# More attention tiles turned by VectorE and DRAM in a hybrid streaming encoder layer, with the halves of the output joined later

## The chip, the cores and the metric

The kernel runs on one core of a Trainium2 chip, in fp32 throughout (TensorE multiplies in the one-pass fp32r format, with every operand split into a high and a low part). The metric is the device time of one execution in microseconds. The profile is that of one execution.

## The reference

One layer of a streaming encoder is computed for a prompt of 1024 frames and a sample chunk of 32 frames, model width 1024. The part that matters here:

```python
u = rmsnorm(h, g_pre) @ w_in
qa, ka, va, ga, qb, kb, vb, gb = jnp.split(u, SPLIT_IDX, axis=-1)
# mixer A, 8 heads of 64: softmax over a band of 8 earlier chunks of 64, with a clipped relative bias
w = jax.nn.softmax(s + bias, axis=-1);  oA = w @ v
# mixer B, 8 heads of 64: stick breaking, strictly causal
w = exp(log_sigmoid(z) + after);        oB = w @ v
y = concat(oA * silu(ga), oB * silu(gb)) @ w_out
h = h + rmsnorm(y, g_post)
h = h + sigmoid(h @ w_ple_gate) * (p @ w_ple)
```

Outputs are the new rows for both groups and the new keys and values.

## The kernel before, in words

**Stages.** First the rows are normalized and turned (`first` stage, to about 40 us). Then come eight stages, one for each pair of heads, in the order A0, B0, A1, B1, A2, B2, A3, B3. In each, the attention of that pair is woven with dense work: the projection columns (`mm_k`, `mm_q`, `mm_v`) of the pair after it, and in the last stage all eight gate columns (`mm_gA`, `mm_gB`). Sample attention runs in stages 2, 3, 6 and 7. After about 600 us the two output products (`o...P`, `g...P`) run, seven half-size products in place of eight.

**One head of attention** (`attention`, L838) has eight query tiles of 128 rows. Tile i of A sees key blocks max(0, i-4) to i (at most 5), tile i of B blocks 0 to i. For each tile, `scores` (L873) multiplies queries by keys (high and low part) into PSUM. For A, a custom VectorE instruction adds the bias and takes the minimum, ScalarE takes the exponential and its row sum, VectorE takes 1/sum, and GpSimd multiplies the row by it (L908 to L910). For B, ScalarE takes two sigmoids, VectorE runs the product scan and GpSimd multiplies. The weights then lie with queries on partitions in a ring called `be`; the product with the values wants keys there. `weights_t` (L919) turns them. Most tiles are turned by TensorE, 128x128 blocks at a time (`ptw`); ScalarE then copies the high part to the ring `wTh` and VectorE subtracts to get the low part in `wTl`. The tiles in `ROUND` (L38), 5 of A and 4 and 6 of B, go round by DRAM instead: VectorE turns 32x32 squares from `be` into the ring `om` (L941), one DMA writes them to a DRAM scratch `swap`, four DMAs read them back into `be` (L946), ScalarE copies the high part and VectorE subtracts (L951, L952). `values` (L969) then multiplies with the value rows for tiles 0-3 and for tiles 4-7 (`PV`); a matmul's moving operand is cut from the ring in runs of 128 elements, one for each tile that sees the block (`Segments`, L166). Its 128 output rows are two halves of 64 that belong together; ScalarE copies one half and VectorE adds the other (L986, L987), and a DMA stores the sum to `o_dr`.

**Gates.** `col_steps` (L770) loads `o_dr` and multiplies it by silu of the gate (L803), in three chunks of 352 columns per gate, and stores to `og_dr`.

**Sums of weights.** `sum_weights` (L1365) forms sums of quarters of the two output weight matrices on GpSimd (tiles named `oB` and `gB` in the profile) and stores them; `SUMS_AT` (L1353) puts them in stages 2, 4, 5 and 6.

**What sets the order.** Every instruction is recorded, then `Recorder.order` (L393) lists them by a simulated schedule: each engine takes the ready instruction with the lowest key; the key is the program position plus an offset from the table `AHEAD_OF` (L28, applied at L351) by engine and name of the tile written. Each engine runs its list strictly in order, and all DMAs are issued by one queue, that of SyncE (SP). All instructions are emitted from L473, so the profile's line is the same for all and the tile names tell them apart. The stream of tiles (`attention_stream`, L1287) emits scores, then two tiles later the turn (`LAG_T`), and the value product with the turn of its last tile (`LAG_V`).

Of the kernel before, what the change touches and what calls it, by code (L numbers as in the profile page):

```python
# [26 lines left out]
NT = 9  # L27
AHEAD_OF = {  # L28
    ('ACT', 'o'): -25, ('ACT', 'oT'): 100, ('ACT', 'w'): -400, ('ACT', 'x'): -75,
    ('DVE', 'newh'): 200, ('DVE', 'sq'): -400, ('POOL', 'bias'): -50, ('POOL', 'kl'): 100,  # L30
    ('POOL', 'ksS'): -50, ('POOL', 'om'): -50, ('POOL', 'qsS'): 100, ('SP', 'be'): 25,
    ('SP', 'biass'): 200, ('SP', 'kl'): 50, ('SP', 'ogg'): -400, ('SP', 'pp'): -400,
    ('SP', 'stv'): -100, ('SP', 'vns'): -25,
# [4 lines left out]
ROUND = {"A": ((5,),), "B": ((4,),(6,))}  # L38
# [127 lines left out]
class Segments:  # L166


    def __init__(self, buf, start, step, n):
        self.buf, self.start, self.step, self.n = buf, start, step, n  # L170
        self.shape = [buf.shape[0], n, P]
        self.box = (buf.box[0], (start, start + (n - 1) * step + P))

    def get(self):
        base = self.buf.get()[:, self.start:self.start + P]
        return bass.AP(tensor=base.tensor, offset=base.offset, ap=[base.ap[0], [self.step, self.n], [1, P]])

    def free(self):
        return self.n * P


class Op:
    __slots__ = ("eng", "what", "args", "kw", "key", "busy", "late", "ready", "left", "after", "at", "size", "shared", "table")
# [89 lines left out]
class Recorder:  # L273


    def __init__(self):
        self.with_table, self.old_table = [], []
        self.ops, self.cls, self.low, self.closed, self.turns = [], 0, 0, [], []
# [31 lines left out]
    def node(self, eng, what, args, kw, after):  # L310
        o = Op()
        o.eng, o.what, o.args, o.kw, o.after = eng, what, args, kw, after
        o.key = (self.cls if eng == "PE" else self.low, len(self.ops))
        o.shared, o.table = False, None
# [3 lines left out]
    def add(self, eng, what, args, kw):  # L318
# [29 lines left out]
        if eng != "PE" and writes:  # L348
            name = str(writes[0].buf.name)
            kind = (eng, name[:next((i for i, x in enumerate(name) if x.isdigit() or x in "AB_"), len(name))])  # L350
            o.key = (o.key[0], o.key[1] + AHEAD_OF.get(kind, 0))  # L351
# [7 lines left out]
    def cost(eng, method, args, kw, writes, reads):  # L359
# [8 lines left out]
        if eng == "ACT":  # L368
            return (165 if psum else 200) + 0.83 * n + (190 if "accum_out" in kw else 0), 0
        if eng == "DVE":  # L370
# [6 lines left out]
            return 155 + 1.04 * n + (83 if method == "tensor_tensor_reduce" else 0), 0  # L377
        if eng == "POOL":
            if method == "tensor_tensor":
                if n == 1:  # L380
                    return 400, 0
                return 190 + (1.77 if out.buf.dtype == F32 else 2.15) * n, 0
# [10 lines left out]
    def order(self):  # L393
# [17 lines left out]
        while len(out) < len(self.ops):  # L411
# [24 lines left out]
            if e == "CTL":  # L436
                done = t
# [41 lines left out]
def stream_step(  # L479
# [22 lines left out]
    o_dr = [scratch([P, T], f"o_dr{n}") for n in range(8)]  # L502
# [34 lines left out]
    ring0, ring1 = Arena(rec, at, "om", 3076), Arena(rec, at, "be", 3640)  # L537
# [126 lines left out]

    KDh, KLD, Lq, V2 = {}, {}, {}, {}
# [104 lines left out]
    def col_steps(j):  # L770
# [7 lines left out]
        def mms(c, part):  # L778
# [20 lines left out]
            if k == "g":  # L799
# [3 lines left out]
                nc.gpsimd.tensor_tensor(sg, sg, box["og"], ALU.mult)  # L803
# [34 lines left out]
    def attention(ab, p, h):  # L838
# [5 lines left out]
        def begin():  # L844
            if ab == "A":
# [4 lines left out]
                box["bias"] = bias  # L850

        def lo_block(i):
            return max(0, i - 4) if ab == "A" else 0

        together = {i: g for g in ROUND[ab] for i in g}
        whole, done_with = {}, []
# [4 lines left out]
        def rooms(i):  # L861

            more = ab == "B"
            g = together.get(i, (i,))
            if g not in whole:
                n = sum(cost(x) for x in g) * P
                whole[g] = ring0.tile([P, n + more * len(g)], f"om{nm}_{i}"), ring1.tile([P, n], f"be{nm}_{i}")
            k, n = g.index(i), cost(i) * P
            a = sum(cost(x) for x in g[:k]) * P
            w0, w1 = whole[g]  # L870
            return w0[:, a + more * k:a + more * k + n + more], w1[:, a:a + n]

        def scores(i):  # L873
# [27 lines left out]
            else:  # L901
# [12 lines left out]

        LAID = {("A", 0): (3, 13), ("A", 1): (4, 20), ("B", 0): (3, 13), ("B", 1): (7, 29)}

        def weights_t(i):  # L919
            g = i // 4  # L920
            step, size = LAID[ab, g]
            if g not in wT:
                wT[g] = [x.tile([P, size * P], f"{x.name}{nm}_{g}") for x in (ringh, ringl)]
            b0 = lo_block(i)
            w0, w1 = state.pop(i)
            n = i + 1 - b0
            at_ = ((i - 4 * g) * step + b0) * P
            hi, lo = (x[:, at_:at_ + n * P] for x in wT[g])
            if i in together:

                group = together[i]
                done_with.append((i, hi, lo))
                if i != group[-1]:
                    return
                w0, w1 = whole[group]
                m = sum(cost(x) for x in group)
# [996 lines left out]
```

## Time and profile before

| | |
|---|---|
| three runs, median (lowest to highest) | 793.03 us (788.52 to 793.21) |
| the profiled execution, span | 790.1 us |
| TensorE busy | 772.5 us (98%) |
| VectorE, ScalarE, GpSimd busy | 599.7, 529.0, 474.9 us |
| mean granted TensorE clock | 0.996 |
| DMA | 154.71 MB, mean 196 GB/s |
| chain that ended last | TensorE 90%, DMA 3%, VectorE 2%, GpSimd 2% |

A row of a group of instructions reads: line, engine, operation, tile written <- tiles read, shapes, count, then the total busy time and the mean time of one, then the idle time of the engine just before them and what ended it. In a timeline a row gives the start, the duration of a merged run of equal instructions and, in brackets, an idle time before it with its releaser. Matmuls overlap in the array, so what one costs is the distance from its start to the start of the next, not its duration.

### The profile page before, as it was taken

The page shows a single profiled execution, that of the slowest core. Times are in us where ns is not written, and L with a number is a line of the kernel's source. Part 1 is how long each engine was busy: PE and PEld are TensorE (multiplying, and loading weights), DVE is VectorE, ACT ScalarE, POOL GpSimd, SP SyncE. Part 2 cuts the span into 40 slices and gives each one's busy share as a digit, 9 for nine tenths or more (in the row PEclk, how much of TensorE's full clock was granted, in tenths as well). Part 3 has the DMA queues.
Part 4 walks back from the last instruction along what each step waited for, and adds up shares of the span by engine and source line. Part 5 has one row for each costly group of instructions (what it writes and reads, how often), then busy time and mean ns, then how long its engine had stood idle before and what let it go on. Part 6 is the DMA issues. An engine that isn't in the chain of part 4 may idle for free.

```text
span 790.1 us, 14436 instructions
## 1 busy us (share of the span) xinstructions
PE 772.5 (98%) x4534; PEld 714.0 (90%) x4534; DVE 599.7 (76%) x1127; ACT 529.0 (67%) x1146; POOL 474.9 (60%) x551
## 2 busy tenths in 40 slices
PE   8999999999999999989999999999999999999997
PEld 7999999999989999979999999999998787888786
DVE  7728757797788888768788788868575587988965
ACT  5647775777677767767767777664446867777651
POOL 5636634574575457757778678566473339599523
PEclk9999999999999999989999999999999999999999
DMA  9646634647676639655857877886489766859754
GB/s 300 227 133 181 142 98 138 148 110 224 162 200 162 158 111 245 165 173 158 226 157 222 196 229 217 211 227 188 142 281 288 244 212 212 271 162 353 268 160 134
DMA packets 184542, 154.71 MB, mean 196 GB/s; under 512 B 64705, under 2 KB 150505, under 8 KB 184466
## 3 DMA queue, kind: packets, MB, share of 16 engines
q1 hardware_dynamic: 184466, 153.79, 66.6%
q8 instruction: 36, 0.59, 0.3%
q14 instruction: 40, 0.33, 0.1%
HBM read 94.97 MB, written 50.36 MB: 184 GB/s over the span
## 4 chain that ended last, share of the span: by engine, by line
PE 90%; DMA 3%; DVE 2%; POOL 2%; SPq 1%; ACT 1%; issue 1%; POOLq 0%; DVEq 0%; ACTq 0%
PE mm_gB L473 6%; PE mm_gA L473 6%; PE mm_qA L473 6%; PE mm_vA L473 6%; PE mm_kA L473 5%; PE mm_vB L473 5%; PE mm_qB L473 5%; PE mm_kB L473 4%; PE PVB L473 4%; PE SB L473 4%; PE PVA L473 3%; PE SA L473 3%; PE ptwB L473 3%; PE g1P L473 2%; PE o3P L473 2%; PE o1P L473 2%
## 5 line engine op out<-in xcount | busy, mean ns | idle before, releaser
L473 POOL TENSOR_TENSOR be<-be,om 128x256 f32<-128x256 f32 (+8 forms) x66 | 81.5, 1238 | 70.4 <-DVE om L473 32.8
L473 DVE TENSOR_TENSOR_SCAN om<-om,SB 128x384 f32<-128x384 f32 (+5 forms) x96 | 92.4, 967 | 20.1 <-ACT be L473 11.9
L473 POOL TENSOR_SCALAR be<-be,statA 128x640 f32<-128x640 f32 (+3 forms) x64 | 46.4, 732 | 38.0 <-DVE statA L473 26.5
L473 ACT ACTIVATE om<-SB 128x384 f32<-128x384 f32 (+5 forms) x96 | 46.8, 499 | 24.9 <-DVE SB L473 14.4
L473 ACT ACTIVATE be<-SB 128x384 f32<-128x384 f32 (+5 forms) x96 | 46.7, 502 | 7.2 <-DVE om L473 6.2
L473 ACT ACTIVATE be<-om,statA 128x640 f32<-128x640 f32 (+3 forms) x64 | 44.5, 696 | 9.1 <-DVE wTl L473 4.2
L473 ACT CAST wTh<-ptwA 128x512 fp32r<-128x512 f32 (+2 forms) x80 | 31.9, 426 | 18.3 <-PE ptwA L473 17.7
L473 DVE TENSOR_TENSOR wTl<-ptwA,wTh 128x512 fp32r<-128x512 f32 (+2 forms) x80 | 37.0, 483 | 8.7 <-ACT wTh L473 8.0
L473 ACT CAST wTh<-ptwB 128x512 fp32r<-128x512 f32 (+3 forms) x64 | 29.9, 491 | 13.2 <-PE ptwB L473 9.1
L473 DVE TENSOR_TENSOR wTl<-ptwB,wTh 128x512 fp32r<-128x512 f32 (+3 forms) x64 | 33.3, 542 | 6.8 <-ACT wTh L473 6.6
L473 PE MATMUL ptwA<-ident,be 128*128 128x128 f32 x200 | 32.3, 273 | 3.8 <-DVE wlsA L473 1.6
L473 DVE TENSOR_TENSOR wTl<-be,wTh 128x640 fp32r<-128x640 f32 (+1 forms) x24 | 28.7, 1196 | 8.3 <-ACT wTh L473 3.5
L473 PE MATMUL SB<-kdB,LB 128*128 128x384 f32 (+5 forms) x96 | 33.4, 353 | 0.0
L473 PE MATMUL SB<-klB,LB 128*128 128x384 f32 (+5 forms) x96 | 32.5, 343 | 0.0
L473 DVE CUSTOM_DVE_ANT_0 om<-SA,biasA 128x320 f32<-128x320 f32 (+2 forms) x64 | 30.1, 480 | 3.0 <-PE SA L473 2.7
L473 POOL TENSOR_TENSOR oB<-oB,oB 128x256 f32<-128x256 f32 x32 | 25.1, 800 | 9.4 <-DMA oB<-in_w_out_dram 9.4
L473 PE MATMUL SA<-kdA,LA 128*128 128x320 f32 (+2 forms) x96 | 30.6, 322 | 0.0
L473 PE MATMUL SA<-klA,LA 128*128 128x320 f32 (+2 forms) x96 | 29.8, 315 | 0.0
L473 PEld LDWEIGHTS ptwA<-ident,be 128*128 128x128 f32 x200 | 24.5, 141 | 5.4 <-issue 3.0
L473 PE MATMUL ptwB<-ident,be 128*128 128x128 f32 x192 | 29.2, 274 | 0.0
L473 POOL TENSOR_TENSOR gB<-gB,gB 128x256 f32<-128x256 f32 x32 | 27.1, 863 | 3.0 <-DMA gB<-in_w_ple_gate_dram 1.5
L473 POOL TENSOR_TENSOR sggB<-sggB,oggB 128x352 f32<-128x352 f32 x12 | 13.9, 1161 | 20.5 <-DVE sggB L473 18.4
(696 smaller groups left out, 2677.9 us busy)
## 6 DMA issues: line engine op xcount, KB each, us to landing
oB<-in_w_out_dram SPq DMA_DIRECT2D x16, 256.0 KB, 4.0
sum_dro<-oB SPq DMA_DIRECT2D x16, 256.0 KB, 2.3
gB<-in_w_ple_gate_dram SPq DMA_DIRECT2D x16, 256.0 KB, 3.8
sum_drg<-gB SPq DMA_DIRECT2D x16, 256.0 KB, 2.4
x<-in_x_prompt_dram SPq DMA_DIRECT2D x16, 256.0 KB, 4.0
h_dr<-h SPq DMA_DIRECT2D x8, 512.0 KB, 3.4
ht<-h_dr SPq DMA_DIRECT2D x8, 512.0 KB, 4.1
raw<-sum_drg SPq DMA_DIRECT2D x16, 256.0 KB, 3.0
```

The costliest lines, as they stand in the source:

```text
L473: getattr(getattr(tc.nc, o.what[0]), o.what[1])(*args, **kw)
```

## The change

**Which tiles go round by DRAM.** `TURNED` names tiles 5, 6 and 7 of A and 4, 5 and 6 of B. Each head now starts with them (`TILES`: A 5, 6, 7, 4, 0-3; B 6, 7, 5, 4, 0-3; the last head still runs 7 down to 0). Tiles are grouped for the value product by `SETS`: A as before, B in (0-3), (4, 5), (6, 7). The value product of a set that ends before the head does is put one tile later (`LAG_G`).

**Landing in place.** The four reads go straight to their place in the ring `wTl`, not to `be`; ScalarE copies the high part from there to `wTh`, and the low part is subtracted in place, on GpSimd (on VectorE in the last pair). For that, the rings hold tiles 4-7 with the 32-element pieces of one partition group side by side, so a matmul's moving operand is cut from the ring in runs of 32 elements. The A softmax works in `be` in place, without `om`.

**Softmax.** A's row sums of a head go to eight columns of a small tile; one reciprocal per head, and one DMA to `one_dr`. The multiplications by 1/sum go away from the tiles.

**Output halves.** Both halves of `PV` (128 rows) are copied and stored, without the VectorE addition. A gate chunk loads two halves and, for A, 1/sum, joins them by one VectorE addition and for A one more GpSimd product.

**Order.** `AHEAD_OF` has one offset per stage for each of 70 kinds, TensorE's among them; `sum_weights` moves to stages 0, 1, 4 and 5, the sample steps are put elsewhere (`SAMPLE_AT`), and a few assumed durations of the order's model change.

Counted over the whole program, TensorE's 128x128 transposes of weights go from 392 to 264; matmuls of `PVB` go from 192 to 288 with the same number of columns; SP's DMA issues go from 840 to 1024.

```diff
-ROUND = {"A": ((5,),), "B": ((4,),(6,))}
+TURNED = {"A": (5, 6, 7), "B": (4, 5, 6)}
+SETS = {"A": ((0, 1, 2, 3), (4, 5, 6, 7)), "B": ((0, 1, 2, 3), (4, 5), (6, 7))}
+TILES = {"A": (5, 6, 7, 4, 0, 1, 2, 3), "B": (6, 7, 5, 4, 0, 1, 2, 3)}
+LAG_G = 1
 AHEAD_OF = {
...
+    ("DVE", "om"): (0, -37, -327, 0, -219, 382, -149, 7, -419, 0),
...
+    ("PE", "PV"): (0, 0, 0, 0, 123, 284, 0, 0, 0, 0),
...
-    o_dr = [scratch([P, T], f"o_dr{n}") for n in range(8)]
+    o_dr = [scratch([2, P, T], f"o_dr{n}") for n in range(8)]
+    one_dr = [scratch([2, SEQ], f"one_dr{p}") for p in range(4)]
...
-                box["og"] = at2.tile([P, CH], F32, tag="bias", name=f"og{kind}{p}_{c}", bufs=2)
-                dma(box["og"], o_dr[n][:, cs])
...
+                for h in range(2):
+                    rows = slice(h * HD, (h + 1) * HD)
+                    dma(og[rows, 0:2], o_dr[n][h, :, cs].rearrange("(a d) t -> d a t", a=2))
+                    if ab == "A" and j not in early:
+                        dma(box["one"][rows, 0:old], one_src(p, h, c * CH, old))
...
-                nc.gpsimd.tensor_tensor(sg, sg, box["og"], ALU.mult)
+                nc.vector.tensor_tensor(og[:, 0], og[:, 0], og[:, 1], ALU.add)
...
+                    nc.gpsimd.tensor_tensor(og[:, 0, 0:old], og[:, 0, 0:old], box["one"][:, 0:old], ALU.mult)
+                nc.gpsimd.tensor_tensor(sg, sg, og[:, 0], ALU.mult)
...
-                nc.scalar.activation(w1[:, 0:n], w0[:, 0:n], AF.Exp, bias=m[:, last:last + 1], scale=-1.0, accum_out=m[:, 3:4])
-                nc.vector.reciprocal(m[:, 3:4], m[:, 3:4])
-                nc.gpsimd.tensor_scalar(w1[:, 0:n], w1[:, 0:n], m[:, 3:4], 1.0, ALU.mult, ALU.mult)
+                one = box["sum"]
+                nc.scalar.activation(w1[:, 0:n], w0[:, 0:n], AF.Exp, bias=m[:, last:last + 1], scale=-1.0, accum_out=one[:, i:i + 1])
+                if i == TILES["A"][-1]:
+                    nc.vector.reciprocal(one, one)
+                    dma(one_dr[p][h].rearrange("(i q) -> q i", q=P), one)
...
-                    dma(w1[32 * c:32 * c + 32].rearrange("k (g x) -> k g x", g=4), x)
...
-                    nc.vector.tensor_tensor(lo, src, f(hi), ALU.subtract)
+                    y = wT[g][1][32 * c:32 * c + 32, at_:at_ + 4 * group].rearrange("k (g y) -> k g y", g=4)[:, :, 0:n * 32]
+                    dma(f(y), x)
+                nc.scalar.copy(hi, f(lo))
+                (nc.vector if (ab, p) == ("B", 3) else nc.gpsimd).tensor_tensor(lo, f(lo), f(hi), ALU.subtract)
...
-                nc.scalar.copy(ot[r], acc[o, c])
-                nc.vector.tensor_tensor(ot[r], acc[r, c], ot[r], ALU.add)
-                dma(o_dr[sidx(ab, p)][r, (4 * g + 2 * x) * P:(4 * g + 2 * x + 2) * P], ot[r])
+                nc.scalar.copy(ot, acc[:, c])
+                dma(o_dr[sidx(ab, p)][h, :, (first + 2 * x) * P:(first + 2 * x + 2) * P], ot)
...
-    SUMS_AT = {2: [('o', 0), ('o', 1)], 4: [('o', 2), ('o', 3)], 5: [('g', 0), ('g', 1)], 6: [('g', 2), ('g', 3)]}
+    SUMS_AT = {0: [('o', 0), ('o', 1)], 1: [('o', 2), ('o', 3)], 4: [('g', 0), ('g', 1)], 5: [('g', 2), ('g', 3)]}
```

The queue of SP in stage 4 before, around the one turned tile of the first head of A2 (`swapA20_5` is its DRAM scratch, `ktB2` and `kdB20`, `klB20` are keys of the next pair, `oB...` quarters for the sums):

```order
L473 DMA swapA20_5_123<-om_165 128x640
L473 DMA out_4_dram<-ktB2_4029 32x32x32
L473 DMA sum_dro_81<-oB122_4039 128x512
L473 DMA kdB20_4193<-kdB20_4193 64x1024
L473 DMA out_4_dram<-ktB2_4029 32x32x32
L473 DMA out_8_dram<-ktB2_4029 32x32 x4
L473 DMA klB20_4195<-klB20_4195 64x1024
L473 DMA be_179<-swapA20_5_123 32x4x160
L473 DMA o_dr2_65<-otA20_0_0_3939 64x256
L473 DMA o_dr2_65<-otA20_0_1_4332 64x256
L473 DMA sum_dro_81<-oB112_4041 128x512
L473 DMA oB212_4382<-in_w_out_dram 128x512
```

and in the changed kernel, the second head of the same pair, from the last output tiles of the first head (`otA20_1`, copied out of its `PV` of tiles 4-7) to the reads of the three turned tiles (`swapA21_5`, `_6`, `_7`):

```order
L550 DMA wr_vA3_0_4509<-in_w_in_dram 128x4x128
L550 DMA o_dr2_65<-otA20_1_0_4317 128x256
L550 DMA o_dr2_65<-otA20_1_1_4370 128x256
L550 DMA wTl_184<-swapA21_5_142 32x4x160 x4
L550 DMA wTl_184<-swapA21_6_143 32x4x160 x2
L550 DMA sum_drg_86<-gB210_4389 128x512
L550 DMA o_dr2_65<-otA20_0_0_4376 128x256
L550 DMA wTl_184<-swapA21_6_143 32x4x160 x2
L550 DMA wTl_184<-swapA21_7_144 32x4x160 x3
L550 DMA o_dr2_65<-otA20_0_1_4616 128x256
```

Before, nine issues stand between the write and the first read, and the other three reads come right behind the rows shown. The reads moved from `be` to `wTl` and now stand behind the stores of the head before; there are twelve of them in a head of A where there were four.

TensorE in stage 5 before, the value product of the first head of B2 for tiles 4-7 (`wTh` and `wTl` moving, `v2B20` loaded as weights; the first rows are the blocks that all four tiles see):

```order
L473 MATMUL PVB20_1_5044<-wTh_644,v2B20_4546 128x512
L473 MATMUL PVB20_1_5044<-wTh_644,v2B20_4546 128x384
L473 MATMUL PVB20_1_5044<-wTh_644,v2B20_4546 128x256
L473 MATMUL PVB20_1_5044<-wTh_644,v2B20_4546 128x128
L473 MATMUL PVB20_1_5044<-wTl_156,v2B20_4546 128x512
L473 MATMUL PVB20_1_5044<-wTl_156,v2B20_4546 128x384
L473 MATMUL PVB20_1_5044<-wTl_156,v2B20_4546 128x256
L473 MATMUL PVB20_1_5044<-wTl_156,v2B20_4546 128x128
```

and in the changed kernel, the same head's product for tiles 4 and 5 (`mm_qA3` is dense work between its parts):

```order
L550 MATMUL PVB20_1_5047<-wTh_672,v2B20_4564 128x256 x5
L550 MATMUL PVB20_1_5047<-wTh_672,v2B20_4564 128x128
L550 MATMUL PVB20_1_5047<-wTl_184,v2B20_4564 128x128
L550 MATMUL mm_qA3_1_5000<-hnl1_172,wh_qA3_1_4683 128x352 x2
L550 MATMUL mm_qA3_2_5099<-hnh2_170,wh_qA3_0_4675 128x352 x4
L550 MATMUL mm_qA3_2_5099<-hnh2_170,wh_qA3_1_4683 128x352 x3
L550 MATMUL PVB20_1_5047<-wTl_184,v2B20_4564 128x256 x5
```

Each matmul now serves two tiles in place of four, tiles 6 and 7 have a product of their own, and the whole high part stands ahead of the low part.

More of the change, by code (lines that the diff above doesn't have):

```diff
@@ L850, in begin @@
                 box["bias"] = bias
+                box["sum"] = small.tile([P, 8], F32, tag="sum", name=f"sum{nm}", bufs=2)
         def lo_block(i):
             return max(0, i - 4) if ab == "A" else 0
-        together = {i: g for g in ROUND[ab] for i in g}
-        whole, done_with = {}, []
+        sets = SETS[ab]
+        set_of = {i: g for g, tiles in enumerate(sets) for i in tiles}
         def cost(i):
@@ L861, in rooms @@
         def rooms(i):
[L863 to L871, printed above, removed]
+            n = cost(i) * P
+            w1 = ring1.tile([P, n], f"be{nm}_{i}")
+            return ring0.tile([P, n + 1], f"om{nm}_{i}") if ab == "B" else w1, w1
         def scores(i):
@@ L1258, in stream_step @@
     pairs = [("A", 0), ("B", 0), ("A", 1), ("B", 1), ("A", 2), ("B", 2), ("A", 3), ("B", 3)]
-    gates = [("gA", p) for p in range(4)] + [("gB", p) for p in range(4)]
-    share = {7: 8}
+    gates = [("g" + x[0], int(x[1])) for x in GATES]
+    early = set()
     order = []
```

219 lines of the change are left out of this document (134 added, 85 removed), and 44 rows, old and new, of the table AHEAD_OF.

## The prediction

> **What bounds the kernel now.** I read the page's busy line first, then the stretches by stage, then who TensorE waits for, and last the timeline around its longest wait.
>
> ```profile
> PE 772.5 (98%) x4534; PEld 714.0 (90%) x4534; DVE 599.7 (76%) x1127; ACT 529.0 (67%) x1146; POOL 474.9 (60%) x551
> ```
>
> ```profile
> 285.00:365.00 80.00, 75.51 (x472) 72.53 (x471) 63.11 (x143) 56.53 (x125) 50.68 (x59) 0.96 0.66 179
> ...
> 480.00:600.00 120.00, 120.00 (x759) 117.83 (x758) 85.54 (x137) 66.62 (x149) 72.32 (x74) 1.00 0.73 212
> ```
>
> TensorE is the bound: busy 98% of the span, and without a gap from 480 to 600 us, while no other engine passes 80% in these stretches. The columns are TensorE, weight load, VectorE, ScalarE, GpSimd, then granted clock, DMA share and GB/s. So an instruction taken from TensorE counts in full, and one moved between the others counts only if TensorE then waits. The stretch 285 to 365 holds the largest hole, and there the clock is 0.96 too. TensorE's waits:
>
> ```profile
> PE PVA L473 <- ACT wTh L473: 2.2, 1, 2.2
> PE ptwA L473 <- DVE wlsA L473: 1.6, 1, 1.6
> PE ptwA L473 <- POOL be L473: 1.3, 1, 1.3
> PE PVA L473 <- DVE wTl L473: 1.2, 1, 1.2
> PE PVB L473 <- ACT wTh L473: 1.1, 1, 1.1
> PE ptwA L473 <- DVE wTl L473: 0.8, 1, 0.8
> ```
>
> Together 8.2 us. Three of the six (2.2, 1.2, 1.1) are value products that wait for the high or low part of a turned tile. What they bring with them stands in the timeline and in one stretch of 10 us:
>
> ```profile
> 338.95 0.32 PE L473 MATMUL mm_vB<-hnh,wl_vB 128*128 128x352 f32 x1
> 341.47 0.85 PE L473 MATMUL PVA<-wTh,v2A 128*128 128x512 f32 x4 [2.19 <-ACT wTh L473]
> ...
> 343.94 1.43 PE L473 MATMUL PVA<-wTl,v2A 128*128 128x512 f32 x4 [1.24 <-DVE wTl L473]
> 345.17 1.38 PE L473 MATMUL PVA<-wTh,v2A 128*128 128x512 f32 x4
> 346.34 1.38 PE L473 MATMUL PVA<-wTl,v2A 128*128 128x512 f32 x4
> ```
>
> ```profile
> 340.00:350.00 10.00, 7.29 (x29) 0.66 0.40 111
> ```
>
> Here the four matmuls from 345.17 take 1.17 us to the next start, where four such take 0.58 elsewhere (row at 410.32 below). The granted clock over these 10 us is 0.66, so 3.4 us are lost beside the 2.2 and 1.2 of waiting: the episode costs 6.8 us. The Trainium skill (TensorE: Matmul & The Clock Gate, section "Why this matters for your kernels") warns of idle gaps above some 3 us, behind which the clock falls; the trace has it already behind two shorter gaps with 0.5 us of work between them. What was late was a round trip, tile 5 of the first head of A2:
>
> ```profile
> 325.55 0.54 SPq L473 DMA_DIRECT2D swapA<-om  x1
> ...
> 332.77 0.58 SPq L473 DMA_DIRECT2D be<-swapA  x1
> ...
> 335.88 1.40 SPq L473 DMA_DIRECT2D be<-swapA  x3
> ```
>
> ```profile
> 340.69 0.72 ACT L473 CAST wTh<-be 128x640 fp32r<-128x640 f32 x1 [2.87 <-DMA be<-swapA]
> ```
>
> From the issue of the write to ScalarE's copy it took 15.1 us, 10.3 of them in SP's queue before the last reads were issued. Round trips are long because of that queue, not of bytes.
>
> **The change part by part.** *Transposes.* 128 leave TensorE (392 to 264). Their price:
>
> ```profile
> 324.76 1.04 PE L473 MATMUL ptwA<-ident,be 128*128 128x128 f32 x8
> 325.55 1.21 PE L473 MATMUL mm_qB<-hnh,wl_qB 128*128 128x352 f32 x6
> 326.61 0.30 PE L473 MATMUL SA<-kdA,LA 128*128 128x320 f32 x1
> ```
>
> Eight start at 324.76 and the next work starts 0.79 us later; that work, six matmuls, then takes 1.06 us where six of its kind take 0.96 (0.16 each), so 0.10 is still the transposes'. (0.79 + 0.10) / 8 = 0.11 us each; the mean of 0.27 in the groups overlaps and is not the price. 128 x 0.11 = **14.1 us less**.
>
> *Value products of B.* 96 matmuls more, with the same columns: per head, tiles 4-7 took 10 matmuls of 512 columns, 2 each of 384, 256 and 128, and now take 24 of 256 and 4 of 128.
>
> ```profile
> 223.54 0.28 PE L473 MATMUL PVsA<-Vh2sA,wlsA 128*128 128x256 f32 x1
> 223.66 0.28 PE L473 MATMUL PVsA<-Vh2sA,whsA 128*128 128x256 f32 x1
> ...
> 410.32 0.74 PE L473 MATMUL PVB<-wTl,v2B 128*128 128x512 f32 x4
> 410.90 0.38 PE L473 MATMUL mm_vA<-hnh,wl_vA 128*128 128x352 f32 x1
> ...
> 425.20 0.39 PE L473 MATMUL SA<-kdA,LA 128*128 128x512 f32 x1
> 425.43 0.40 PE L473 MATMUL SA<-klA,LA 128*128 128x512 f32 x1
> ```
>
> 256 columns with weights of their own go at 0.12 us; 512, 384, 256 and 128 together at 0.58, that is 0.45 ns a column like the 0.23 for 512. By columns alone nothing is added; if each of the 96 showed the 0.05 us by which a transpose of 128 columns (0.11) stands above its columns (0.06), it would be 5 us. The sample rows are of exactly the new size and show no such gap, so I take 1 us, between 0 and 5.
>
> *The moving operand in runs of 32.* No row has it. Runs of 128 (410.32) cost no more per column than an unbroken row (425.20). I take 0. If it halved the rate, the columns concerned are 2560 for each half and head of A and 3328 of B, over 16 halves each: 94,208 x 0.45 ns = 42 us. The Trainium skill (SBUF — State Buffer, section "Door 1: The DMA port swizzle") says that full rate needs two accesses to a line of 16 bytes, which a run of 128 bytes gives; by that rule it is 0 as well, and no run yet shows it.
>
> *VectorE and GpSimd.*
>
> ```profile
> L473 DVE TENSOR_TENSOR wTl<-ptwA,wTh 128x512 fp32r<-128x512 f32 x32 | 21.7, 682 | 7.0 <-ACT wTh L473 6.7
> L473 DVE TENSOR_TENSOR wTl<-be,wTh 128x640 fp32r<-128x640 f32 x16 | 17.4, 1085 | 3.4 <-DMA kdB<-kdB 3.3
> L473 DVE STREAM_TRANSPOSE om<-be 128x640 f32<-128x640 f32 x16 | 13.3, 833 | 0.2
> L473 DVE TENSOR_TENSOR otA<-PVA,otA 64x256 f32<-64x256 f32 x32 | 12.3, 417 | 14.7 <-ACT otA L473 12.7 <-PE ptwA L473 1.1 <-DMA out_dram<-vtB 0.8
> ```
>
> ```profile
> L473 POOL TENSOR_SCALAR be<-be,statA 128x640 f32<-128x640 f32 (+3 forms) x64 | 46.4, 732 | 38.0 <-DVE statA L473 26.5
> ```
>
> ```profile
> L473 POOL TENSOR_TENSOR wl_qB<-wr_qB,wh_qB 128x512 fp32r<-128x512 f32 x8 | 12.1, 1524 | 3.4 <-issue 3.1
> ```
>
> VectorE loses 64 output additions (64 x 0.39 = 25 us), all but 6 of the 24 subtractions of turned tiles (about 21) and 24 of 512 columns (16); it gets 24 more turns (16 x 0.83 + 8 x 1.0 = 21) and 24 gate additions (0.5 each by the columns of the output additions, 12): some 30 us less. GpSimd loses the 64 scalings (46 us) and gets 42 subtractions at 1.5 us per 512 columns (30 x 1.9 + 6 x 2.3 + 6 x 2.7 = 87) and 12 gate products of about 1 us: some 53 us more, 528 in all. ScalarE changes 24 copies of 512 columns for 24 of 640 or 768: nothing. None becomes the bound; TensorE's own work covers them, and with TensorE waiting they would cost their length. What stays on a path is latency. For A, 1/sum and the scaling (0.9 us for 640 columns by the mean above, and what they queue behind) leave the way to the turn; at its end a subtraction of 1.9 us stands in place of 1.1, but the whole high part of the product is multiplied meanwhile (1.1 us for A) and covers the difference.
>
> *DMA.*
>
> ```profile
> swapA<-om SPq DMA_DIRECT2D x8, 320.0 KB, 2.6
> ...
> be<-swapA SPq DMA_DIRECT2D x32, 80.0 KB, 2.5
> ...
> oggA<-o_dr SPq DMA_DIRECT2D x12, 176.0 KB, 2.6
> ```
>
> Round trips go from 24 to 48: 16 x 320 + 8 x 384 KB more each way, and 4 MB more each way for the halves, about 26 MB. SP issues 184 more; at 0.4 to 0.5 us (1.40 for three above) that is some 85 us of queue more, spread over the stages. Average room is there (DMA share 0.66 in the worst stretch); single trips are what may be late. The gates' extra loads are issued with a chunk's first matmul; its 24 matmuls of 0.16 us cover the 2.6 us. Were they late, VectorE's new addition would hold the scans of B3 queued behind it, a microsecond or two in each of 24 chunks, which TensorE's dense work in that stretch hides.
>
> *Waits.* 8.2 us listed and 3.4 of clock, 11.6 in all; 7.9 (2.2 + 1.2 + 3.4 + 1.1) are round trips. Bounds: all gone, -11.6; as often late per trip, with twice the trips, +7.9. The turned tiles now come first in a head and A's scaling no longer stands before the turn; against that, twelve reads of a head of A share one queue. I take **-4**.
>
> Sum: -14.1 + 1 - 4 = -17.1, the span from 790.1 to 773.0. The median of the runs shown is 2.9 us above that span, so I forecast 776.
>
> **The rivals.** *All waits go* (the new order keeps every part ready): 793.0 - 13.1 - 11.6 = 768. For it: only six waits exist. Against it: the sample steps and scans that cause four of them remain.
>
> *Trips as often late as before:* 793.0 - 13.1 + 7.9 = 788. For it: the late trip above came from SP's queue, which gets longer.
>
> *Landing in place blocks* (the other side). The reads land in the ring from which the head before is still being multiplied; 20 + 13 blocks of a head of A fill its 33. In the order of the changed kernel the reads of the next head stand behind the stores of that product, and SP's queue is strict, so a late product delays twelve reads, and these the next product. Price 6.8 us each time, as measured; the trips' 7.9 of now are replaced. It makes the kernel slower than before from the fourth such place of 16 (21.0 / 6.8 = 3.1). With five: 793.0 - 13.1 - 7.9 + 34 = 806. Against it: the order sets turned tiles' scores well ahead of their product.
>
> *Runs of 32 slow the moving operand:* 776 + 42 = 818; it makes the kernel slower than before once 17.1 of the 42 appear. Against it: nothing in the rows but the free runs of 128.
>
> *It does not do what it says* (another engine's chain takes the freed time): 793. Against it, the chain that ended last:
>
> ```profile
> PE 90%; DMA 3%; DVE 2%; POOL 2%; SPq 1%; ACT 1%; issue 1%; POOLq 0%; DVEq 0%; ACTq 0%
> ```
>
> Only 10% of it lies outside TensorE.
>
> **How the numbers follow.** Forecast 0.45 (alone 770 to 783), all waits go 0.20, as often late 0.18, landing blocks 0.06, runs of 32 0.04, nothing 0.07. A measurement tells about 1% from no change, that is below 785 or above 801. Faster: 0.45 + 0.20 + 0.08 (the part of the late case that ends under 785) = 0.73; slower: 0.06 + 0.04 = 0.10; same: 0.10 + 0.07 = 0.17. The range leaves out the two slow cases and the far ends: 764 to 790.
>
> **What would show it.** Right: 264 transposes at the same spacing; `PVB` of 256 columns starting 0.12 us apart; TensorE's listed waits at most 8 us and the clock at 1.00 in every stretch but one; VectorE near 570 and GpSimd near 520 us. Wrong: `PV` matmuls of 512 columns more than 0.25 us apart (runs of 32), or many value products waiting for `wTl` or `wTh` with clocks under 0.9 behind them (landing).

## The result, and the profile after

The changed kernel takes **865.64 us** (median; 862.3 to 873.19), where the kernel before took 791.36 beside it: a ratio of 1.0957 [1.09, 1.1015]. It is slower by 74 us; the forecast was 776. The profiled execution has a span of 860.5 us and a mean clock of 0.962.

The busy times, the main DMA queue (packets, MB, share of 16 engines) and the chain that ended last, after:

```profile
PE 787.6 (92%) x4502; PEld 724.3 (84%) x4502; DVE 563.6 (65%) x989; ACT 523.5 (61%) x1122; POOL 506.1 (59%) x541
...
q1 hardware_dynamic: 220690, 181.36, 80.5%
...
PE 48%; DMA 17%; DVE 6%; SPq 6%; ACT 3%; issue 3%; POOL 1%; ACTq 0%; DVEq 0%; POOLq 0%
```

VectorE and ScalarE are where the prediction put them (about 570 us, and no change from 529.0), GpSimd is 22 us below its sum of 528, and 32 matmuls fewer run on TensorE (4534 before). But TensorE holds only 48% of the chain (90% before), and DMA 17%. What TensorE waits for (us in total, times, longest):

```profile
PE PVA L550 <- ACT wTh L550: 26.3, 5, 8.4
PE SB L550 <- DVE om L550: 8.5, 3, 5.9
PE ptwA L550 <- DVE wTl L550: 6.5, 1, 6.5
PE SB L550 <- DMA klB<-klB: 5.8, 2, 4.5
PE mm_kA L550 <- ACT stvB L550: 4.1, 1, 4.1
```

The six listed waits of before came to 8.2 us; here the first row alone has 26.3. One of its five, in TensorE's, ScalarE's and SP's timeline:

```profile
94.33 1.29 PE L550 MATMUL mm_qB<-hnh,wh_qB 128*128 128x352 f32 x7
103.98 2.61 PE L550 MATMUL PVA<-wTh,v2A 128*128 128x512 f32 x8 [8.37 <-ACT wTh L550]
```

```profile
103.20 0.72 ACT L550 CAST wTh<-wTl 128x640 fp32r<-128x640 f32 x1 [9.61 <-DMA wTl<-swapA]
```

```profile
83.37 0.36 SPq L550 DMA_DIRECT2D swapA<-om  x1
83.83 1.43 SPq L550 DMA_DIRECT2D one_dr<-sumA  x1
...
86.52 1.08 SPq L550 DMA_DIRECT2D swapA<-om  x2
87.69 0.81 SPq L550 DMA_DIRECT2D sum_dro<-oB  x1
88.55 1.16 SPq L550 DMA_DIRECT2D biasA<-r_dr  x1
96.58 2.70 SPq L550 DMA_DIRECT2D wTl<-swapA  x4
```

TensorE waits for a turned tile, but that is the end of the story: SP issues nothing from 89.71 to 96.58. The reads of the tile are the next in its queue, and they need the tile's write, issued at 83.37, to have landed. What is in flight then shows in the DMA view from 80 to 100 us (40 slices of 0.5 us) and its list of issues (KB each, median us to landing):

```profile
DMA  9999999999747999596999989979599799999999
GB/s 219 336 383 292 167 233 223 213 251 310 256 55 65 236 30 12 6 9 11 26 30 37 28 29 40 28 19 46 29 100 76 90 218 339 310 215 278 306 316 300
...
swapA<-om SPq DMA_DIRECT2D x3, 320.0 KB, 13.7
...
one_dr<-sumA SPq DMA_DIRECT2D x1, 4.0 KB
```

From 87 to 94 us the DMA engines are shown busy and move 6 to 46 GB/s. The three writes of turned tiles take 13.7 us to land by the median (the eight of `swapA` before: 2.6). The store of 1/sum, `one_dr`, stands among them: 4 KB only, but in 1024 runs of 4 bytes, since it is stored across its partitions. There are eight (SP's instructions on this tile, ns min/median/max, first and last start). SP's own waits name them too, as what landed last before SP went on:

```profile
L550 SPq DMA_DIRECT2D one_dr<-sumA x8: 379/464/1426, 83.8 to 519.9; - x8
```

```profile
SPq L550 <- DMA one_dr<-sumA: 21.1, 7, 6.9
```

The eight longest gaps of TensorE (8.5, 6.6, 4.2, 6.1, 4.7, 4.3, 5.1 and 8.4 us, at 95, 121, 226, 273, 378, 395, 491 and 524 us) each come 4 to 14 us behind the start of one of the eight stores. Only the first, third, seventh and eighth are value products that wait for `wTh`; the others are transposes that wait for `wTl` (121 us), scores that wait for `om` or for keys, and a projection that waits for a copy. Eleven stretches run at half the clock, 64.9 us in all, and eight of them begin inside these gaps; TensorE is busy in 47 of the 64.9 us, so some 23 are lost beside the gaps.

### The profile page after: what moved, and what is told of

The parts are those of the page before. It is cut to its first block, busy times and chain, and to the rows that moved or that the text cites. A ratio compares the mean times of both kernels' runs of the same rounds, so it can differ in the third digit from the quotient of the medians.

```text
span 860.5 us, 14501 instructions
## 1 busy us (share of the span) xinstructions
PE 787.6 (92%) x4502; PEld 724.3 (84%) x4502; DVE 563.6 (65%) x989; ACT 523.5 (61%) x1122; POOL 506.1 (59%) x541
## 2 busy tenths in 40 slices
DMA packets 220767, 182.28 MB, mean 212 GB/s; under 512 B 76865, under 2 KB 183657, under 8 KB 220690
## 4 chain that ended last, share of the span: by engine, by line
PE 48%; DMA 17%; DVE 6%; SPq 6%; ACT 3%; issue 3%; POOL 1%; ACTq 0%; DVEq 0%; POOLq 0%
SPq L550 6%; DMA wTl<-swapA 5%; PE mm_vA L550 4%; PE mm_kB L550 4%; PE mm_kA L550 3%; PE PVB L550 3%; PE PVA L550 3%; PE SB L550 2%; PE o0P L550 2%; DMA swapB<-om 2%; PE o1P L550 2%; PE g2P L550 2%; PE mm_vB L550 2%; PE g3P L550 2%; PE SA L550 2%
## 5 line engine op out<-in xcount | busy, mean ns | idle before, releaser
L550 POOL TENSOR_TENSOR wTl<-wTl,wTh 128x640 fp32r<-128x640 f32 (+2 forms) x42 | 71.4, 1709 | 65.3 <-ACT wTh L550 46.9
L550 POOL TENSOR_TENSOR be<-be,om 128x1024 f32<-128x1024 f32 (+8 forms) x66 | 86.8, 1323 | 35.8 <-DVE om L550 24.7
L550 ACT CAST wTh<-wTl 128x640 fp32r<-128x640 f32 (+2 forms) x48 | 37.5, 782 | 44.8 <-DMA wTl<-swapA 36.1
L550 DVE STREAM_TRANSPOSE om<-be 128x640 f32<-128x640 f32 (+2 forms) x48 | 43.1, 901 | 15.8 <-POOL be L550 9.3
L550 ACT ACTIVATE be<-be,statA 128x640 f32<-128x640 f32 (+2 forms) x64 | 44.3, 694 | 10.3 <-DVE statA L550 10.2
L550 DVE TENSOR_TENSOR wTl<-ptwA,wTh 128x512 fp32r<-128x512 f32 (+3 forms) x48 | 23.0, 484 | 41.5 <-ACT wTh L550 21.5
L550 PE MATMUL PVA<-wTh,v2A 128*128 128x512 f32 (+3 forms) x96 | 23.5, 393 | 26.3 <-ACT wTh L550 26.3
L550 PEld LDWEIGHTS PVA<-wTh,v2A 128*128 128x128 f32 x96 | 21.3, 249 | 29.6 <-ACT wTh L550 27.7
L550 PE MATMUL SB<-kdB,LB 128*128 128x384 f32 (+5 forms) x96 | 33.7, 355 | 8.5 <-DVE om L550 8.5
L550 DVE CUSTOM_DVE_ANT_0 be<-SA,biasA 128x320 f32<-128x320 f32 (+2 forms) x64 | 29.8, 477 | 14.2 <-PE SA L550 6.1
L550 DVE TENSOR_TENSOR SB<-SB,maskb 128x128 f32<-128x128 f32 x64 | 17.6, 290 | 25.1 <-PE SB L550 24.5
L550 POOL TENSOR_TENSOR oB<-oB,oB 128x256 f32<-128x256 f32 x32 | 24.7, 792 | 15.0 <-DMA oB<-in_w_out_dram 13.6
```

Source lines behind the costliest of these rows:

```text
L550: getattr(getattr(tc.nc, o.what[0]), o.what[1])(*args, **kw)
```

## The experiments

Ratios are to the kernel before, run beside each. e1 is an edit of the changed kernel, e11, e12 and e13 are edits of the kernel before, and all others are edits of e1. Each edit is planned anew by the recorder, so the order moves a little with it. e4, another form of e11, gave no time. e5, e14 and e15 leave A's softmax undivided.

**First question: is it the stores in runs of 4 bytes?**

*e1.* VectorE turns the sums (in a tile widened to 32 columns), so that a head's 1/sum is stored in rows of 128 bytes:

```diff
-                    dma(one_dr[p][h].rearrange("(i q) -> q i", q=P), one)
+                    rows = small.tile([P, 32], F32, tag="rows", name=f"rows{nm}", bufs=2)
+                    nc.vector.transpose(rows, one)
+                    for c in range(4):
+                        dma(one_dr[p][h].rearrange("(i q) -> i q", q=P)[:, 32 * c:32 * c + 32], rows[32 * c:32 * c + 8])
```

> The changed kernel, but 1/sum is stored in runs of 128 bytes: VectorE turns the small tile in 32x32 squares, and four DMAs of 8 partitions store it (12 more DMA issues per pair of heads) in place of one DMA of 1024 runs of 4 bytes. Theory 1 (the eight stores in runs of 4 bytes hold up all DMA engines for some 10 us each, and every round trip behind them comes late): the eight largest waits of TensorE go (48 us) and with them most of the half clock (27 us), so 775 to 792 us. Rival 1 (landing in place behind one queue makes the trips late): 845 to 875. Rival 2 (26 MB more and 184 more issues make all transfers late): 845 to 875, since nothing of that goes away.

Measured: 806.2 us (804.74 to 807.87), 1.0203 [1.016, 1.0246]; 59 us are back. Its busy times and TensorE's two longest groups of waits:

```profile
PE 769.9 (96%) x4502; PEld 708.2 (88%) x4502; DVE 566.6 (71%) x997; ACT 523.4 (65%) x1122; POOL 506.4 (63%) x549
```

```profile
PE SA L550 <- DVE om L550: 2.9, 1, 2.9
PE SB L550 <- DVE om L550: 2.8, 2, 1.8
```

The long waits for turned tiles are gone, and landing in place is untouched. The two spans differ by 57.5 us: by the busy lines, 39.8 of them are idle time of TensorE and 17.7 are the same 4502 matmuls taking longer. It is still 14 us over its upper expectation.

*e2* and *e3* add to e1 a store of the same values to a scratch that nothing reads, in 1024 runs of 4 bytes, in e2 side by side as in the change, in e3 each 512 bytes from the next:

```diff
 e2:
+                    dma(scratch([2, SEQ], f"more{nm}")[h].rearrange("(i q) -> q i", q=P), one[:, 0:8])
 e3:
+                    dma(scratch([P, 8, P], f"more{nm}")[:, :, 0:1].rearrange("q i x -> q (i x)"), one[:, 0:8])
```

> The kernel of the run before, with the store in runs of 4 bytes added again, to a scratch that nobody reads. Theory 1: back to 850 to 880 us, with a wait of TensorE of 4 to 9 us behind each of the eight stores. Both rivals: as the run before it, within 1%.

> As the run before it, but each 4 bytes land 512 bytes from the next, so that no two of them share a line of DRAM. If it is the number of small writes that costs: as the run before it, 850 to 880 us. If it is that many engines write parts of the same line: near the first run, 775 to 800.

Measured: e2 875.44 us, 1.1083 [1.1028, 1.1138], 69 over e1, 8.7 for each store; e3 817.6, 1.0357 [1.03, 1.0413], 11 over e1, 1.4 each, between its two expectations. The number of packets is the same in both (q1: 221202), so most of the cost is not their number but that they lie side by side. Why that costs, no run shows.

*e11* adds such a store to the kernel before, and *e12* is its control:

```diff
+                if i == 7:
+                    dma(scratch([SEQ], f"more{nm}").rearrange("(i q) -> q i", q=P), w1[:, 0:8])
```

> The kernel before, with one more store per head of A, 1024 runs of 4 bytes side by side in DRAM (eight weights of the last tile, to a scratch that nothing reads); nothing else is changed. The store in runs of 4 bytes costs the same wherever it stands (8.7 us each in the changed kernel): 791 + 70 = 861, at least 840. If it only hurts where turned tiles land in place: 795 to 815. If it was the wait for 1/sum by the gates: no change.

> The kernel before, planned with the rule for equal keys that the other additions to it use (the earlier instruction first), and nothing else: the control for the two kernels that add DMAs to the kernel before. Both theories: within 1% of the kernel before, 785 to 798 us. More than that, and the additions have to be compared with this one instead.

Measured: control 791.05 us, 1.0003 [0.9975, 1.0031]; with the stores 851.51, 1.0776 [1.0709, 1.0843]: 60 us, 7.6 each, in a kernel that has nothing of the change. The second of the eight stores in SP's queue, the DMA view from 95 to 115 us, and the largest group of TensorE's waits in e11:

```profile
102.88 0.38 SPq L473 DMA_DIRECT2D moreA<-be  x1
```

```profile
DMA  1008998999999899789690310195784469366767
GB/s 25 9 0 188 205 131 279 279 203 277 311 315 352 259 253 204 203 119 37 132 51 10 6 1 1 3 68 49 35 32 30 27 28 54 19 50 64 92 109 176
```

```profile
PE PVA L473 <- ACT wTh L473: 24.9, 7, 5.9
```

The picture is close to that of the change: 1 to 68 GB/s from 105.5 to 113.5 us, and value products waiting for turned tiles. The engines are not shown busy all through it, though: from 105.5 to 108 us, where least is moved, their share is under 0.4.

**Second question: why is e1 not at 776?** From the median spacing of each shape of matmul I worked out how much TensorE work each kernel has left at a time. What is left in the kernel before, less what is left in the variant, is its lead in us. It begins with the difference of the whole work (758.1 us before; 751.8 in e1, 750.0 in e5, 752.3 in e7, 765.4 in e8), and what changes it later are waits and a slow clock. How the shapes are grouped moves a row by up to 8 us at its left end, and by under 3 us from 450 us on:

```
at us     100   300   450   500   520   560   620   640   750
e1        5.1   2.4   7.0   7.1   1.6  -4.9  -5.9 -10.5 -12.5
e5        6.6   2.2   2.8   3.8   0.2  -0.2  -2.4  -4.7  -4.7
e7        2.0 -19.7 -15.4 -18.1 -19.1 -19.5 -19.3 -19.3 -23.1
e8       -8.0  -2.7   4.9   6.1   4.7  -0.6  -1.3  -1.7 -17.8
```

So until 500 us e1 keeps the work that it saves, to within some 3 us, and in sum waits neither more nor less than the kernel before. From there it loses 20, 12 of them by 560, where the gates of A load two halves and 1/sum. TensorE's columns of the stretch 480 to 560, before and in e1:

```profile
480.00:560.00 80.00, 80.00 (x510) 77.99 (x509) 62.06 (x103) 48.65 (x112) 49.26 (x56) 1.00 0.73 206
```

```profile
480.00:560.00 80.00, 71.30 (x436) 68.01 (x435) 59.82 (x98) 40.45 (x94) 50.85 (x56) 0.96 0.88 224
```

And SP's queue in that stretch of e1, where a gate's load is issued in 0.60 us:

```profile
499.28 0.53 SPq L550 DMA_DIRECT2D swapB<-om  x1
499.86 0.60 SPq L550 DMA_DIRECT2D oggA<-o_dr  x1
500.50 0.61 SPq L550 DMA_DIRECT2D oggA<-one_dr  x1
...
506.62 0.38 SPq L550 DMA_DIRECT2D o_dr<-otB  x1
507.09 1.90 SPq L550 DMA_DIRECT2D wTl<-swapB  x4
```

*e5, e6, e7* take the change apart at the gates; *e8* has the tiles of the kernel before (and transposes them by TensorE again):

```diff
 e5, no loads of 1/sum:
-                        dma(box["one"][rows, 0:old], one_src(p, h, c * CH, old))
...
-                    nc.gpsimd.tensor_tensor(og[:, 0, 0:old], og[:, 0, 0:old], box["one"][:, 0:old], ALU.mult)
+                    nc.gpsimd.tensor_tensor(og[:, 0, 0:old], og[:, 0, 0:old], og[:, 1, 0:old], ALU.mult)
 e6, halves joined before the store:
-                nc.scalar.copy(ot, acc[:, c])
+                nc.scalar.copy(ot[r], acc[(1 - h) * HD:(2 - h) * HD, c])
+                nc.vector.tensor_tensor(ot[r], acc[r, c], ot[r], ALU.add)
 e7, e6 and 1/sum on the tiles:
+                nc.gpsimd.tensor_scalar(w1[:, 0:n], w1[:, 0:n], m[:, 3:4], 1.0, ALU.mult, ALU.mult)
 e8, tiles as before:
-TURNED = {"A": (5, 6, 7), "B": (4, 5, 6)}
+TURNED = {"A": (5,), "B": (4, 6)}
```

> The kernel with 1/sum stored in rows (806.2 us), and its gates of A no longer load 1/sum: the 24 loads of 80 or 88 KB (2.0 MB) are gone, and the GpSimd product takes the second half in their place (the softmax of A is left undivided). In that kernel TensorE loses 12 us at 500 to 550 us and 6 us at 600 to 650, where the gates run, its DMA engines are 0.87 to 0.91 busy there, and a gate's load of the halves lands after 4.7 us where it took 2.4. Theory A (the gates' own loads fill the DMA queues and hold up the work that is late at 500 to 650 us): a third of the gates' extra reads goes, so 797 to 803 us. Theory B (the round trips of the last two heads and the order are what is late): 804 to 809.

> The kernel with 1/sum stored in rows, and its output halves are joined before the store again, as in the kernel before (64 VectorE additions of 64x256, one half stored, one half loaded by the gates); 1/sum is still loaded by the gates. 4.2 MB of stores in the stages and 4.3 MB of loads in the gates go; VectorE gets 13 us of work more, 25 for the additions less 12 in the gates. Theory A: the gates' DMA falls by two thirds of what was added, 790 to 798 us. Theory B: 803 to 809, and more if VectorE's additions hold up its queue.

> Turned tiles, landing in place and the new order alone: halves are joined before the store, and 1/sum is multiplied into each tile by GpSimd as in the kernel before, so that the gates load what they loaded before and nothing of 1/sum is stored. Theory A: nothing of the gates' loads is left, TensorE's loss at 500 to 650 us (18 us) goes almost whole, and the transposes' gain shows: 776 to 788 us, below the kernel before. Theory B: 800 to 812, since GpSimd gets 46 us of work and each turned tile of A stands 0.9 us behind a scaling.

> The kernel with 1/sum stored in rows, with only tile 5 of A and tiles 4 and 6 of B turned by VectorE and DRAM, as in the kernel before; the others go by TensorE again, 128 transposes of 0.11 us (14 us). The order, the layout and the gates stay as changed. Theory A: the gates' loads still hold up the same place, and the transposes come on top: 812 to 820 us, less what the lighter DMA of the stages gives back. Theory B: the round trips' lateness goes with 24 of 48 trips: 794 to 804.

Measured: e5 794.86 us, 1.0062 [1.0032, 1.0092]; e6 826.97, 1.0438 [1.038, 1.0496]; e7 812.36, 1.0264 [1.0228, 1.0301]; e8 814.48, 1.0292 [1.0259, 1.0324]. The loads of 1/sum are worth 11 us, as theory A had it and more. The other three do not bear it out: e6 lies above both theories' numbers, e7 at the upper end of theory B's, and e8 in theory A's range, but by a loss behind the gates. In e7, with the gates as before, the lead changes by 4 us only from 480 (-15.3) to 700 (-19.2):

```profile
480.00:560.00 80.00, 77.43 (x497) 73.82 (x496) 63.50 (x118) 53.12 (x121) 49.47 (x57) 1.00 0.81 221
```

so the loss there needs the gates' loads. But e7 loses 22 us between 100 and 300 us instead, where the longest of these waits stands:

```profile
PE PVA L550 <- ACT wTh L550: 11.1, 4, 8.3
```

and e6 loses about 24 there; neither theory names that place. e8 shows the transposes' price: its work is 13.6 us more than that of e1, for 128. It gains 14 us on the kernel before from 100 to 500 us, so with fewer round trips this order does wait less there; it loses 8 at the gates (500 to 640 us) and 16 after 640. Its gates load all that those of e1 load, where e1 loses 18: so by this run the loss there needs the round trips as well.

*e9, e14, e15* ask by what the 24 loads of 1/sum cost. e9 loads 1/sum once for a gate (8 loads of 256 KB); e14 loads, in place of 64 copies of one row, 64 rows of the output; in e15 the loads stay and the product does not read them:

```diff
 e9:
+                    if ab == "A" and c == 0:
...
+                        dma(box["one"][rows], one_src(p, h, 0, SEQ))
 e14:
+                        dma(box["one"][rows, 0:old], o_dr[n][h, 0:HD, c * CH:c * CH + old])
 e15:
+                    nc.gpsimd.tensor_tensor(og[:, 0, 0:old], og[:, 0, 0:old], og[:, 1, 0:old], ALU.mult)
```

> The kernel with 1/sum stored in rows, and each gate of A loads 1/sum once for its three chunks: 8 loads of 256 KB in place of 24 of 80 or 88 KB, the same bytes. Leaving out all 24 took 11 us. Theory A1 (what cost was their issues in SP's queue: a gate's load is issued in 0.60 us by the median, 24 of them in 14 us): 16 issues fewer, 796 to 801 us. Theory A2 (what cost was their 2 MB on the DMA engines, 0.87 to 0.91 busy there): 804 to 810.

> The kernel with 1/sum stored in rows, whose gates of A load, in place of 64 copies of one row of 1/sum, 64 rows of the head's output, with the same bytes, partitions and number of DMAs (the gates of A then multiply by an output half instead of 1/sum). Theory A2 (bytes): 803 to 810 us, as with 1/sum. Theory A3 (64 reads of one DRAM row cost, as writes of 4 bytes beside each other do): 793 to 799, as without the loads.

> The kernel with 1/sum stored in rows and all its gate loads, but the GpSimd product in the gates of A multiplies by the second half instead of 1/sum, so that nothing waits for the 24 loads of 1/sum. Theory C1 (GpSimd's product waits for the load, and the products of the last B heads stand behind it in GpSimd's queue): 793 to 799 us, as without the loads. Theory C2 (the loads stand ahead of the last B heads' round trips in SP's queue, 0.60 us each): 803 to 809.

Measured: 806.47 us (1.0208 [1.017, 1.0246]), 803.86 (1.0163 [1.0101, 1.0225]) and 806.88 (1.0208 [1.0149, 1.0266]). Fewer issues, other rows, no reader: none gives the 11 us back, e9 and e14 come out as theory A2 (bytes) had it, e15 as theory C2 (SP's queue). Left were the bytes, and SP's queue. Against the bytes stands that the DMA engines of e5, without these loads, are as busy from 480 to 560 us (0.90, where e1 has 0.88).

*e13* adds 6.3 MB of copies to the kernel before, in its code at the gates; *e17* and *e18* let ScalarE issue the loads of 1/sum, and all gate loads:

```diff
 e13:
+                for more in range(2 if kind[1] == "A" else 1):
+                    dma(scratch([P, CH], f"more{kind}{p}_{c}_{more}"), o_dr[n][:, cs])
 e17:
+    dma_act = nc.scalar.dma_start
...
-                        dma(box["one"][rows, 0:old], one_src(p, h, c * CH, old))
+                        dma_act(box["one"][rows, 0:old], one_src(p, h, c * CH, old))
```

> The kernel before, planned as the control, and at each gate's load of an output chunk further copies of that chunk from DRAM to DRAM that nothing waits for: two for each chunk of A, one for each of B, 36 of 176 KB, 6.3 MB, about what the changed gates load more (4.2 MB of halves and 2.0 MB of 1/sum). Theory A (the gates' traffic alone holds up what runs beside it): 10 to 18 us over the control. Theory B (the loss comes from the changed order, and the traffic only shows there): within 4 us of the control.

> The kernel with 1/sum stored in rows, its 24 loads of 1/sum issued by ScalarE instead of SyncE: same bytes, same waits, SP's queue 24 issues (14 us) shorter. If the 11 us are SP's queue: 794 to 800 us. If they are bytes on the DMA engines, or chance of the order: 803 to 810. ScalarE's queue grows by about 14 us, idle there before.

> As the one before, with the loads of the halves (48 of 176 KB) issued by ScalarE too. If SP's queue is what costs: 785 to 796 us, TensorE busy in 480 to 560 us over 77 of 80 (71 with all loads on SP). If not: 803 to 812; above that, ScalarE's copies wait behind 43 us of issues.

Measured: e13 786.53 us, 0.9939 [0.9911, 0.9967]; e17 817.31, 1.034 [1.03, 1.0381]; e18 815.31, 1.0319 [1.0272, 1.0367]. In e13 TensorE is still busy all through the stretch:

```profile
480.00:560.00 80.00, 80.00 (x507) 78.27 (x506) 61.15 (x97) 46.30 (x105) 50.08 (x51) 1.00 0.78 211
```

But this does not test the gates' traffic. Nothing waits for the copies, so the order put most of them far ahead of the gates (count, issue time in ns, first and last start):

```profile
L475 SPq DMA_DIRECT2D moregA<-o_dr x24: 469/528/928, 105.7 to 495.2; - x24
L475 SPq DMA_DIRECT2D moregB<-o_dr x12: 500/550/1614, 167.1 to 573.0; - x12
```

Ten of the 36 start after 480 us, 1.8 MB, and the DMA share of the stretch is 0.78, where e1 has 0.88. What e13 shows is that 6.3 MB more, spread over the stages, cost nothing. (It is even 0.6% faster: it gains 7 us between 300 and 350 us, where the kernel before has its largest hole; the control gains 5 there.) A shorter queue on SP does not help either; e17 loses 11 us between 500 and 520. But e17 lies above both its expectations and e18 above its upper one, and the loads now stand in ScalarE's queue, so these two do not say what SP's queue costs. The Trainium skill (DMA: Bandwidth & Descriptors, section "Issuing engines are not separate DMA queues") says that issuing from another engine saves only issue time; here not even that showed in the kernel's time.

*e10* and *e16* change the order alone: the 18 offsets of the kernel before (its table put in as well), and the changed kernel's offsets planned with landings 2 us later.

```diff
 e10:
-            o.key = (o.key[0], o.key[1] + (AHEAD_OF[kind][STAGES.index(self.stage)] if kind in AHEAD_OF else 0), o.key[2])
+            o.key = (o.key[0], o.key[1] + (AHEAD_OF.get(kind, 0) if eng != "PE" else 0), o.key[2])
 e16:
-DMA_NS, DMA_RATE, DMA_MARGIN = 1500, 320.0, 2000
+DMA_NS, DMA_RATE, DMA_MARGIN = 1500, 320.0, 4000
```

> The kernel with 1/sum stored in rows, with the 18 offsets of the order's table of the kernel before in place of the 70 kinds by stage. Theory A (what is left over the forecast lies in the DMA of the gates; the order matters little): 800 to 812 us. Theory B (each stage's time hangs on the hand-set order, which is why removing work elsewhere did not help): 820 to 860.

> The kernel with 1/sum stored in rows, planned with every DMA assumed to land 2 us later (a gate's load lands 4.7 to 6 us after its issue in the profile, the plan assumed about 3.5 behind the queue), so that the order puts other work ahead of what waits for a landing. If the lost time is waits for landings that the order could cover: 785 to 800 us. If the order is near the best that such offsets give: 803 to 830, since the offsets were set for the other assumption.

Measured: 838.9 us (836.94 in the runs that the ratio is of), 1.0572 [1.0508, 1.0636], and 848.58, 1.0743 [1.0717, 1.0769]. e10 is as its theory B had it, e16 above both its expectations. These orders cost 31 and 42 us over e1, more than any part of the gates.

**What is settled and what is open.** Settled: 59 of the 74 us are the eight stores in runs of 4 bytes; taken away they go, and added to two other kernels they come. Of the other 15, the place is known: e1 loses 18 us from 500 to 640, where the gates load. e7 without these loads loses 4 from 480 to 640, and e8, with them but with half the round trips, loses 8 from 500 to 640: by these two runs it takes both. By themselves, one row read 64 times, the wait for 1/sum and the number of issues in SP's queue do not account for it. The bytes of the gates' loads are not ruled out, since e13 put few of its copies there. How the order of the last stage fits these loads is not ruled out either: e10 and e16 show that the order can do as much. No run parts these two. No version beat the kernel before but e13, whose gain falls ahead of the gates and has nothing of the change in it.

## Why the prediction was wrong

*Transposes, -14.1.* Right: 264 run, 0.109 us apart; by median spacing they take 28.8 us where 42.7 were, and e8 against e1 gives 13.6.

*Value products of B, +1 (0 to 5).* Right. At full clock, each shape of `PVB` at its median spacing, B's products take 33.7 us before, 34.7 in e1, e5 and e9 and 35.7 in the changed kernel: 1 to 2 more.

*Runs of 32: nothing.* Right; matmuls of 256 columns cut in runs of 32 stand 0.120 us apart (median), the sample rows of that size 0.118.

*VectorE and GpSimd.* Right in kind: 563.6 (about 570 forecast) and 506.1 (520 to 528), and neither became the bound. GpSimd's 42 subtractions take 71.4 us where 87 were reckoned.

*DMA.* This is the step that failed. It counted bytes (26 MB forecast, 27.57 measured: 154.71 before, 182.28 after) and issues, and found room on the average. For that it took a share of 0.66 as the worst stretch, though its own row for the gates has 0.73; e1 has 0.88 there. But the larger miss is another: the eight stores of 1/sum, 4 KB each, added nothing to either count, and their form, one element to a run, stood in the diff it read. No row of before had such a store, so its cost should have been bounded; the prediction gave it none. It measured 7.4 to 8.7 us each (59, 60 and 69 us for eight, in e1, e11 and e2). The Trainium skill says it (DMA: Bandwidth & Descriptors, section "Rules for kernel authors"): a last dimension that is not contiguous becomes one descriptor per element, and should be rearranged. The trace agrees on the count: e2 has 8320 packets more than e1, 1040 for each store of 1024 elements. But e3, with as many, shows that the count is not the price.

*Waits, -4 (-11.6 to +7.9).* Wrong by sign and far outside its bounds. The gaps of TensorE over each shape's median spacing, slow clock included, come to about 97 us after, 23 before, and 45 in e1. So without the stores it is still more than +20: the "gates' extra loads" that TensorE's dense work was to hide are the place where most of that is lost.

*Landing in place blocks (806).* Its signs came: clocks below 0.9 at eight places, value products waiting for `wTh` at four of them, and near its 6.8 us each (59 / 8 = 7.4). But the ring was not the cause: e1 lands in place as well, and the places are gone. That e1 takes just 806 is chance. The signs told where TensorE stands, and not what is late; that took the DMA view.

*The price of an episode, 6.8.* It counts part of one wait twice. The clock had already fallen when the wait of 1.24 us began, at 342.7 us, so it fell behind one gap of 2.2 us, not two; between the two waits stand six matmuls, some 0.9 us of work and not 0.5. In the slow 6.8 us TensorE is busy for 5.6, so 2.8 are lost, and the episode costs 6.2.

*All waits go*, *as often late* and *nothing* all put the end at 793 or below, and e1 lies above that too. *Runs of 32* (818) did not come: see its row above.

## What to carry to other kernels

Price every DMA that a change adds by its runs, not by its bytes: a store across partitions to adjacent 4-byte places is the most expensive 4 KB in this kernel, and a 32x32 transpose on an engine with room makes rows of it. When a product waits for a tile that went by DRAM, look at the GB/s row, and not only at the busy share of the DMA engines, before blaming queue or ring. In a kernel planned by hand-set offsets, an edit can move waits to other places by more than it is worth itself (e6 and e7 lose over 20 us far from what they edit), so its parts have to be judged by stretch (who leads, where), and not by the end alone. And before a null result is read, look where the added instructions ran: the copies of e13 ran mostly elsewhere.

## What the runs showed of the hardware

1024 writes of 4 bytes side by side in DRAM hold all DMA of the core down: to 6 to 46 GB/s for 7 us in the changed kernel, with the engines shown as busy, and to 1 to 68 GB/s for 8 us in e11. They delay transfers that have nothing to do with them (320 KB landed after 13.7 us, where 2.6 was usual), and cost 7.4 to 8.7 us of kernel time. The same 1024 writes with neighbouring partitions 4 KB apart cost 1.4 us of kernel time (e3), and rows of 128 bytes in four DMAs had no such hole behind them (e1). Reading one row into 64 partitions cost what 64 rows cost (806.2 against 803.9 us). In e1 TensorE was busy for 3.3 of the 5.8 us behind 510 us, with no single idle stretch over 1.8 us, and the granted clock was 0.50 in the 6.75 us behind that.
